# A 31-tap depthwise convolution on three engines or on TensorE, with its modulations moved the other way

## The chip, the cores and the metric

The kernel runs on one core of a Trainium2 chip. The metric is the device time of one execution in microseconds (us), the median of several runs. Five engines work side by side, each on its own instruction stream in order: TensorE (PE; its weight loads are shown apart as PEld), VectorE (DVE), ScalarE (ACT), GpSimd (POOL) and SyncE (SP), which here does nothing but issue DMAs. Instructions wait for each other by semaphores.

## The reference, cut to what matters

The program is a two-layer decoder trunk: 256 tokens, 2048 channels, float32. Layer 0 mixes tokens with a convolution module, layer 1 with attention; each is followed by a gated feed-forward block. The change concerns layer 0's mixer and the modulations around it.

```python
shift, scale, gate = jnp.split(silu(c) @ w + b, 3)          # adaLN, w is 2048 x 6144
h = rms_norm(x, g) * (1.0 + scale) + shift
u = h @ pw1_w + pw1_b                                       # 2048 -> 4096
val, gt = jnp.split(u, 2, axis=-1)
u = val * sigmoid(gt)
u = causal_depthwise_conv(u, dw_w, dw_b)                    # 31 taps, per channel
u = silu(layer_norm(u, ln_g, ln_b))
x = x + gate * (u @ pw2_w + pw2_b)
```

## The kernel before, in words

Activations lie channels on partitions, tokens along the row: 16 tiles of 128 x 256. A product keeps 128 x 128 blocks of weights stationary and streams 256 tokens. Float32 accuracy comes from splitting: ScalarE rounds a weight piece to a high part `wh` (L213), VectorE subtracts to get a low part `wl` (L214), and TensorE takes three products per block, `wh`\*`hh`, `wh`\*`hl`, `wl`\*`hh` (L251, L252, L253), at the fast fp32r rate. A piece is 8 blocks, 512 KB. `pieces` (L217) loads and splits ahead: after the first 16 pieces of pw1, five pieces of loads and three of splits.

All loads go through one queue on SyncE in the order in which the program writes them (`load`, L194). The buffers set when each can be issued: six for raw pieces (`raw`), three of 1 MB for modulation weights (`mraw`).

pw1 has 64 pieces. In the first 16 (called the head here) eight output blocks run at once, one piece for each channel tile kt. Each kt needs its scale and shift first: two 1 MB loads, two sums on VectorE over rows of 2048 (L276), then the modulated tile and its two parts (`start_tiles`, L498; `modulate_tile`, L354). GpSimd also rebuilds a full float32 tile `hf` (L506). The other 48 pieces run one output block after another, value and gate blocks of a tile in turn, so 4 pieces finish a tile. Of these 48, every fourth is "plain": not split, one float32 product a block (L249) on `hf`.

When a tile is finished, `pw1_done` (L517) computes `u` and starts a convolution (`conv`, L531), a generator that is advanced between pieces. Of the 31 taps, 12 are multiplied by ScalarE (L541) and added by GpSimd (L543, L545), 18 are multiply-adds on VectorE into a PSUM bank (L549), one is ScalarE's start (L535); VectorE joins both sums (L552). `y_sum` and `y_square` (L560, L579) give mean and variance over channels by products with a constant matrix (L569, L583).

Between the pieces run the steps of `mods0` (L482), the modulations that come next: the gate of this mixer, then scale and shift of the feed-forward. `mod_rows` (L455) sums them on TensorE, 1 MB a step, four products of 32 columns by 512 at a time (L466); only the last 1 MB loads go to VectorE (`mod_part`, L289). The rate is 0.6 steps a piece in pw1 (L31) and in pw2.

After pw1 the LayerNorm ends (L600 to L626): the last convolutions, the last sums, then pw2 (256 blocks) can start.

Of the kernel before, what the change touches and what calls it, by code (L numbers as in the profile page):

```python
# [17 lines left out]
PB = 8  # 128x128 blocks of weights in a piece  # L18
# [7 lines left out]
PRODUCTS = 8       # buffers between ScalarE and GpSimd  # L26
# [10 lines left out]
def plan(nbs, kts, first, stagger=4):  # L37
    """Order of the (output block, contraction tile) pairs of a product."""
# [9 lines left out]
class Cfg:  # L48
    def __init__(self, D, T, H, F, CW, FW):
# [3 lines left out]
        self.GH = 4  # L53
        self.rows0 = min(ROWS, KD // 4 - 1)

# [15 lines left out]
        items = [("c", KD), ("mix_g0", KD), ("mix_b0", 3 * KD), ("pw1_b", 2 * KD), ("cdw", KD * CW), ("cdb", KD), ("ln_g", KD), ("ln_b", KD),  # L71
# [6 lines left out]
        pl["pw1"] = plan(pairs, kd, min(8, 2 * KD), 0)  # L78
# [29 lines left out]
def hybrid_trunk(ctx: ExitStack, tc: tile.TileContext, cfg: Cfg, io: dict):  # L108
# [28 lines left out]
    # ---------------------------------------------------------------- constants and activations  # L137
# [53 lines left out]
    plain = {("pw1", i) for i in range(KD, 4 * KD) if i % PLAIN[0] == PLAIN[1]} if KD > 8 else set()  # L191
# [13 lines left out]
    def split_next():  # L205
        """High and low parts, of 12 significant bits each, of the next piece of weights."""
        blocks, v, n = raws[len(parts)]
        if stream[len(parts)] in plain:
            parts.append((blocks, v, None))
            return  # L210
# [6 lines left out]
    def pieces(name):  # L217
        """The pieces of a plan; loads and splits run ahead, over the ends of the plans."""
# [15 lines left out]
    def gemm(name, xh, xl, done, after=None, banks=(), x=None, width=None):  # L234
        """Weights stationary: psum[128 outputs, T] for each output block; done(block, psum)."""
        set_rate(name)
        left, ps, banks = {}, {}, list(banks)
        for nb, _ in cfg.plans[name]:
            left[nb] = left.get(nb, 0) + 1
        for blocks, wh, wl in pieces(name):  # L240
            for b, (nb, kt) in enumerate(blocks):
                first = nb not in ps
                if first:
                    ps[nb] = (banks.pop(0) if banks else psum_acc)()
# [3 lines left out]
                if wl is None:  # L248
                    nc.tensor.matmul(o, wh[:, c], x[kt], start=first, stop=left[nb] == 0)  # L249
                else:  # L250
                    nc.tensor.matmul(o, wh[:, c], xh[kt], start=first, stop=False)  # L251
                    nc.tensor.matmul(o, wh[:, c], xl[kt], start=False, stop=False)  # L252
                    nc.tensor.matmul(o, wl[:, c], xh[kt], start=False, stop=left[nb] == 0)  # L253
# [113 lines left out]
    class Entry:  # L367
# [585 lines left out]
```

## Time and profile before

| | |
|---|---|
| runs (3), us | 2379.94, 2383.69, 2388.55 |
| median | 2383.69 us |
| span of the profiled execution, first to last instruction | 2373.7 us |
| median less that span | 10.0 us |
| instructions | 45095 |
| TensorE busy / weight loads | 2280.7 / 2194.9 us |
| VectorE, ScalarE, GpSimd busy | 1814.1, 1219.0, 335.1 us |
| bytes moved by DMA, mean rate | 603.62 MB, 254 GB/s |

The profile holds one execution; the time of a run also contains some 10 us before the first and after the last instruction. A group row reads: line, engine, operation, output<-inputs, shapes, count, then busy time and mean duration of one instruction in ns, then the idle time before them and what ended it. A timeline row reads: start, length, engine, line, operation, count of merged instructions. A float32 product of TensorE appears as two records, an fp32r product as one. Matmuls overlap in the pipeline, so what one costs is the step from start to start, not its duration. A window row gives busy time and count of each engine, then the clock granted to TensorE, the busy share of the DMA engines and the rate.

### The profile page before, as it was taken

The numbers are of one execution on the slowest core, as the hardware profiler recorded it, in microseconds if no ns is written. First come the engines' busy times: TensorE is split into PE (matmuls) and PEld (weight loads), VectorE is DVE, ScalarE is ACT, GpSimd is POOL, SyncE is SP. The second block draws the span as 40 slices with busy tenths as digits, with TensorE's granted clock in tenths as the row PEclk, the third lists the DMA queues.
The fourth block names the chain that finished last, engine by engine and source line by source line (L and its number), as shares of the span: only waits on it lengthen the run. The fifth ranks groups of instructions, "written<-read, shape, count | busy, mean of one in ns | idle before, by whom it ended". The sixth has DMA issues, their size and how long they took to land.

```text
span 2373.7 us, 45095 instructions
## 1 busy us (share of the span) xinstructions
PE 2280.7 (96%) x18228; PEld 2194.9 (92%) x18228; DVE 1814.1 (76%) x2470; ACT 1219.0 (51%) x1828; POOL 335.1 (14%) x357
## 2 busy tenths in 40 slices
PE   5689989999999999999999999999999999999997
PEld 4677859999999999999998999999999999999997
DVE  8978988898878788788887667789876555666644
ACT  3266667665553345555465544556555434555443
POOL 2368652300000000000121000121000000000011
PEclk8799999999999999999999999999999999999999
DMA  8987879677769877778866676676865555566663
GB/s 341 350 342 279 299 261 354 209 264 282 274 249 354 311 275 291 265 278 322 317 239 241 240 254 238 239 250 260 292 216 187 187 187 187 187 188 187 188 186 105
DMA packets 138308, 603.62 MB, mean 254 GB/s; under 512 B 15346, under 2 KB 15474, under 8 KB 113522
## 3 DMA queue, kind: packets, MB, share of 16 engines
q1 hardware_dynamic: 138098, 600.74, 71.5%
q8 instruction: 142, 2.33, 0.4%
q14 instruction: 68, 0.55, 0.1%
HBM read 598.58 MB, written 2.10 MB: 253 GB/s over the span
## 4 chain that ended last, share of the span: by engine, by line
PE 82%; DVE 10%; issue 2%; POOL 2%; DMA 2%; ACT 2%; DVEq 0%; SPq 0%; POOLq 0%; ACTq 0%
PE ps L252 25%; PE ps L251 25%; PE ps L253 25%; DVE mraw L276 3%; DVE wl L214 2%; POOL y L545 2%; DMA mraw<-in_mt_ffn 1%; PE ps L787 1%; PE ps L788 1%; PE ps L789 1%; PE ps L249 1%; DVE auxb L549 1%; PE auxa L466 1%; DVE t L363 0%; DVE hl L321 0%
## 5 line engine op out<-in xcount | busy, mean ns | idle before, releaser
L213 ACT CAST wh<-raw 128x1024 fp32r<-128x1024 f32 x740 | 773.8, 1048 | 884.9 <-PE ps L252 652.1
L214 DVE TENSOR_TENSOR wl<-raw,wh 128x1024 fp32r<-128x1024 f32 x740 | 910.2, 1234 | 379.0 <-ACT wh L213 372.0
L251 PE MATMUL ps<-hh,wh 128*128 128x256 f32 (+1 forms) x3696 | 1036.6, 284 | 49.2 <-ACT hh L320 48.1
L252 PE MATMUL ps<-hl,wh 128*128 128x256 f32 (+1 forms) x3696 | 1044.1, 283 | 4.0 <-DVE hl L318 2.0
L253 PE MATMUL ps<-hh,wl 128*128 128x256 f32 (+1 forms) x3696 | 1039.0, 281 | 6.3 <-DVE wl L214 6.3
L251 PEld LDWEIGHTS ps<-hh,wh 128*128 128x128 f32 x3696 | 694.2, 190 | 63.0 <-ACT hh L320 52.5
L252 PEld LDWEIGHTS ps<-hl,wh 128*128 128x128 f32 x3696 | 709.2, 192 | 9.3 <-issue 3.4
L253 PEld LDWEIGHTS ps<-hh,wl 128*128 128x128 f32 x3696 | 704.2, 191 | 11.5 <-DVE wl L214 7.3
L252 PE MATMUL ps<-gl,wh 128*128 128x256 f32 x1408 | 396.2, 281 | 0.0
L251 PE MATMUL ps<-gh,wh 128*128 128x256 f32 x1408 | 396.2, 281 | 0.0
L253 PE MATMUL ps<-gh,wl 128*128 128x256 f32 x1408 | 396.2, 281 | 0.0
L276 DVE CUSTOM_DVE_ANT_0 mraw<-mraw,csr 128x2048 f32<-128x2048 f32 x152 | 347.6, 2287 | 56.2 <-DMA mraw<-in_mt_ffn 34.8
L336 POOL TENSOR_TENSOR sumsq<-sumsq,t 128x256 f32<-128x256 f32 x56 | 70.2, 1254 | 1570.4 <-ACT t L332 1570.1
L252 PEld LDWEIGHTS ps<-gl,wh 128*128 128x128 f32 x1408 | 265.0, 188 | 0.0
L251 PEld LDWEIGHTS ps<-gh,wh 128*128 128x128 f32 x1408 | 265.0, 188 | 0.0
L253 PEld LDWEIGHTS ps<-gh,wl 128*128 128x128 f32 x1408 | 265.0, 188 | 0.0
L656 DVE SCALAR_TENSOR_TENSOR t<-ps,par,t 128x254 f32<-128x254 f32 x336 | 160.4, 479 | 4.1
L545 POOL TENSOR_TENSOR y<-y,prod 128x256 f32<-128x256 f32 x160 | 144.4, 911 | 12.9 <-ACT prod L541 3.0
L549 DVE SCALAR_TENSOR_TENSOR auxb<-u,cpar,auxb 128x256 f32<-128x256 f32 x288 | 118.8, 481 | 1.1 <-ACT auxb L535 0.9
L541 ACT ACTIVATE prod<-u,cpar 128x256 f32<-128x256 f32 x192 | 85.5, 500 | 40.3 <-DVE u L528 24.1
L653 ACT ACTIVATE t<-ps,par 128x256 f32<-128x256 f32 x168 | 93.9, 560 | 0.0
L332 ACT ACTIVATE t<-x 128x256 f32<-128x256 f32 x75 | 30.1, 414 | 85.9 <-DVE x L676 37.0
(174 smaller groups left out, 2107.9 us busy)
## 6 DMA issues: line engine op xcount, KB each, us to landing
raw<-in_w_down SPq DMA_DIRECT2D x176, 512.0 KB, 4.3
mraw<-in_mt_mix SPq DMA_DIRECT2D x80, 1024.0 KB, 7.3
mraw<-in_mt_ffn SPq DMA_DIRECT2D x72, 1024.0 KB, 6.7
raw<-in_w_pw SPq DMA_DIRECT2D x96, 512.0 KB, 6.2
raw<-in_w_up01b SPq DMA_DIRECT2D x84, 512.0 KB, 4.9
raw<-in_w_up11b SPq DMA_DIRECT2D x84, 512.0 KB, 3.5
raw<-in_w_up00b SPq DMA_DIRECT2D x80, 512.0 KB, 4.6
raw<-in_w_up10b SPq DMA_DIRECT2D x80, 512.0 KB, 3.6
```

Source lines behind the costliest of these rows:

```text
L213: nc.scalar.copy(wh[:, :n], v[:, :n])
L214: nc.vector.tensor_tensor(wl[:, :n], v[:, :n], wh[:, :n].bitcast(F32), op=ALU.subtract)
L251: nc.tensor.matmul(o, wh[:, c], xh[kt], start=first, stop=False)
L252: nc.tensor.matmul(o, wh[:, c], xl[kt], start=False, stop=False)
L253: nc.tensor.matmul(o, wl[:, c], xh[kt], start=False, stop=left[nb] == 0)
L276: nc.vector.tensor_tensor_reduce(out=v, in0=v, in1=csr, scale=1.0, scalar=0.0, op0=ALU.mult, op1=ALU.add, accum_out=macc[:, nb:nb + 1])
L336: engine.tensor_tensor(self.sum, self.sum, sq, op=ALU.add)
L541: nc.scalar.activation(pr, u[:, i:i + T], AF.Copy, scale=tap(i))
L545: nc.gpsimd.tensor_tensor(y, y, pr, op=ALU.add)
L549: nc.vector.scalar_tensor_tensor(o, u[:, k:k + T], tap(k), o, op0=ALU.mult, op1=ALU.add)
L653: nc.scalar.activation(y, ps[:, :T], AF.Identity, bias=pc(f"fdb{i}", nb, 1), scale=w(FW - 1))
L656: nc.vector.scalar_tensor_tensor(y[:, s:], ps[:, :T - s], w(k), y[:, s:], op0=ALU.mult, op1=ALU.add)
```

## The change

The convolution moves to TensorE. For each channel tile the 128 channels are cut into four blocks of 32; for block i a buffer `wide` holds four copies of its `u`, each on 32 partitions and shifted by 0 to 3 tokens. One product with a 128 x 32 matrix of taps then does four taps of 32 channels; eight such products, 4 tokens apart, do the 31 taps (one tap is zero), and the four blocks go to the four column groups of the array: 32 float32 products of 128 x 32 by 256 a tile, 512 in all. The copies are made by DMA: 16 issues for each group of two tiles (the last two tiles are groups of one), on the same SyncE queue, in program order. GpSimd builds the tap matrices, ScalarE adds the bias while it copies the result out.

In return the modulations go to VectorE: all of `mods0` but 8 steps runs as `mod_part`, at 1.06 steps a piece instead of 0.6. No piece of pw1 is plain any more, so `hf` is gone. Value and gate of a tile share one PSUM bank (`gemm_pairs`). In the head, GpSimd multiplies x by 1/rms for all tiles in advance and ScalarE applies scale and shift, where VectorE did both in one instruction.

```diff
-POOL_TAPS = 12     # conv taps that ScalarE multiplies and GpSimd adds; VectorE has the others
-CONV_PACE = 0.7    # steps of the running convolutions after each piece
-PLAIN = (4, 3)     # of each 4 pieces of pw1, the one that goes to TensorE as float32, unsplit
-PW1_RATE, BUBBLE, LN_STEPS = 0.6, 8, 7
+HEAD = 8
+SH = 4
+CONV_PACE = 1.25
+PW1_RATE, BUBBLE, LN_STEPS = 1.06, 8, 7
...
+                mm = [(wh, xh), (wh, xl), (wl, xh)]
+                for k, (w, x) in enumerate(mm):
+                    nc.tensor.matmul(o, w[:, c], x[kt], start=first and k == 0, stop=left[j] == 0 and k == 2,
+                                     skip_group_check=True)
...
         def mods0():
-            yield from mod_rows("mix0", 2 * KD // 4, KD // 4)
+            yield from mod_part("mix0", 2)
             nc.vector.tensor_tensor(gb, modv["mix0"][:, 2 * KD:3 * KD], pc("pw2_b"), op=ALU.mult)
-            have.add(("mix0", 2))
-            yield from mod_rows("ffn0", KD // 4, KD // 4)
-            mod_scale("ffn0", 0, KD)
-            have.add(("ffn0", 1))
+            yield from mod_part("ffn0", 1)
             if cfg.rows0:
                 yield from mod_rows("ffn0", 0, cfg.rows0)
             yield from mod_part("ffn0", 0, 4 * cfg.rows0)
...
+        for kt in range(KD):
+            nc.gpsimd.tensor_tensor(ys[kt], xs[kt], rs, op=ALU.mult)
...
-                hh[kt], hl[kt] = modulate_tile("mix0", kt, rs)
-                nc.gpsimd.tensor_tensor(hf[kt], hh[kt].bitcast(F32), hl[kt].bitcast(F32), op=ALU.add)
+                hh[kt], hl[kt] = [v[:, :T] for v in h_tiles(kt)]
+                t = t256()
+                nc.scalar.activation(t, ys[kt], AF.Identity, bias=modv["mix0"][:, kt:kt + 1],
+                                     scale=moda["mix0"][:, kt:kt + 1])
+                split_act(t, hh[kt], hl[kt])
...
+        def conv(g, u):
+            n = len(g)
+            v = wide[groups.index(g) % 2]
+            for s in range(SH):
+                for i in range(SH):
+                    load(u[i * C32:(i + 1) * C32, :n, :], v[s * C32:(s + 1) * C32, i, :n, PADW - s:PADW - s + T])
+            taps = []
+            for j in g:
+                t = cpool2.tile([P, SH * NM, C32], F32, name="taps", bufs=3)
+                w = pc("cdw", j * SH * NM, SH * NM)
+                nc.gpsimd.tensor_tensor(t, w.unsqueeze(2).to_broadcast([P, SH * NM, C32]),
+                                        pc("eye").unsqueeze(1).to_broadcast([P, SH * NM, C32]), op=ALU.mult)
+                taps.append(t)
+            yield
+            yield
+            for a, j in enumerate(g):
+                o = psum_b()[:, :T]
+                for m in range(NM):
+                    for i in range(SH):
+                        nc.tensor.matmul(o[i * C32:(i + 1) * C32, :], taps[a][:, i * NM + m, :],
+                                         v[:, i, a, SH * m:SH * m + T], start=m == 0, stop=m == NM - 1,
+                                         tile_position=(0, i * C32))
+                    if m == NM // 2 - 1:
+                        yield
+                nc.scalar.activation(ys[j], o, AF.Identity, bias=pc("cdb", j, 1))
+                late.append(j)
+                yield
```

How the instructions stand. First SyncE at the end of the head, before: behind the last modulation loads and the parameters come five raw pieces at once (`mt` are modulation weights that VectorE sums, `mr` those that TensorE sums).

```order
L195 DMA mraw<-in_mt_mix 128x2048 x2
L195 DMA raw<-in_w_pw 128x1024
L195 DMA par<-in_params 128x912
L195 DMA cst<-in_consts 128x144
L195 DMA raw<-in_w_pw 128x1024 x5
L195 DMA mraw<-in_mr_mix 128x2048
L195 DMA raw<-in_w_pw 128x1024 x2
```

The same place on SyncE in the changed kernel:

```order
L194 DMA mraw<-in_mt_mix 128x2048 x2
L194 DMA raw<-in_w_pw 128x1024
L194 DMA par<-in_params 128x912
L194 DMA cst<-in_consts 128x144
L194 DMA wide_218<-u 32x2x256 x16
L194 DMA wide_219<-u 32x2x256 x16
L194 DMA mraw<-in_mt_mix 128x2048
L194 DMA raw<-in_w_pw 128x1024 x5
```

The 32 copies of the first two groups, which read `u` and so wait for the end of the head's products, now stand ahead of the five raw pieces.

Second, SyncE of the changed kernel at the end of pw1 (names with their buffer numbers; `wide1` takes tile 14, `wide0` tile 15, the last):

```order
L194 DMA raw_3031<-in_w_pw1 128x1024
...
L194 DMA wide1_219<-u_3129 32x256 x16
L194 DMA mraw_3168<-in_mt_ffn0 128x2048
L194 DMA raw_3172<-in_w_pw2 128x1024
L194 DMA mraw_3203<-in_mt_ffn0 128x2048
L194 DMA raw_3206<-in_w_pw2 128x1024
L194 DMA mraw_3253<-in_mt_ffn0 128x2048
L194 DMA raw_3256<-in_w_pw2 128x1024
L194 DMA mraw_3303<-in_mt_ffn0 128x2048
L194 DMA raw_3307<-in_w_pw2 128x1024
L194 DMA wide0_218<-u_3337 32x256 x16
```

Between the last weights of pw1 (the first row) and the copies of the last tile stand five modulation loads of 1 MB and five pieces of pw2 (one of each in the two rows left out); before, no DMA stood between the last tile of pw1 and its convolution.

Third, TensorE of the changed kernel after the head, where before the split products ran on with a four-product modulation step about every second piece (`hh`, `hl` and `wl` as above, `taps` the tap matrices):

```order
L268 MATMUL ps<-hh_561,wl 128x256
L568 MATMUL auxb<-wide_218,taps 32x256 x32
L591 MATMUL ps<-y_186,ones_d 128x256
L568 MATMUL auxb<-wide_219,taps 32x256 x2
L568 MATMUL auxb<-wide_218,taps 32x256
L568 MATMUL auxb<-wide_219,taps 32x256
L568 MATMUL auxb<-wide_218,taps 32x256 x4
L568 MATMUL auxb<-wide_219,taps 32x256 x29
L568 MATMUL auxb<-wide_218,taps 32x256 x11
L568 MATMUL auxb<-wide_219,taps 32x256 x5
L268 MATMUL ps<-hh_606,wh 128x256
```

After one piece behind the head, 85 convolution products come in a block; later groups come as blocks of 64, three to five pieces behind the end of their tiles.

More of the change, by code (lines that the diff above doesn't have):

```diff
@@ L53, in __init__ @@
         self.GH = 4
+        self.NM = -(-CW // SH)
         self.rows0 = min(ROWS, KD // 4 - 1)
@@ L531, in conv @@
[L531 to L553 removed]
+        groups = [list(range(j, min(j + 2, KD - 2))) for j in range(0, KD - 2, 2)] + [[KD - 2], [KD - 1]]
@@ new lines, in hybrid_trunk, with pw1_done @@
+        group_of = {j: g for g in groups for j in g}
+        wide = [cpool2.tile([P, SH, 2, PADW + T], F32, name=f"wide{i}") for i in range(2)]
+        for v in wide:
+            nc.gpsimd.memset(v[:, :, :, :PADW], 0.0)
+            nc.gpsimd.memset(v[:, :, :, PADW + T - SH + 1:], 0.0)
+        u_of = {}
+        def pw1_done(j, ps):
+            g = group_of[j]
+            if j == g[0]:
+                u_of[j] = cpool2.tile([P, 2, T], F32, name="u", bufs=5)
+            u = u_of[g[0]][:, j - g[0], :]
+            sg = t256()
+            nc.scalar.activation(sg, ps[:, T:2 * T], AF.Sigmoid, bias=pc("pw1_b", j + KD, 1))
+            nc.vector.scalar_tensor_tensor(u, ps[:, :T], pc("pw1_b", j, 1), sg, op0=ALU.add, op1=ALU.mult)
+            if j == g[-1]:
+                side.append(conv(g, u_of.pop(g[0])))
```

110 lines of the change are left out of this document (39 added, 71 removed).

## The prediction

> **What bounds the kernel now.** I read the page's busy times first, then the windows, cut at the borders of layer 0's stages, then the groups of TensorE and VectorE in each stage, then timelines where one operation's price is needed.
>
> ```profile
> PE 2280.7 (96%) x18228; PEld 2194.9 (92%) x18228; DVE 1814.1 (76%) x2470; ACT 1219.0 (51%) x1828; POOL 335.1 (14%) x357
> ```
>
> TensorE bounds the whole; the change touches only the first 455 us. The window rows are the head, the other 48 pieces of pw1 (the stage below), the gap to pw2, and pw2:
>
> ```profile
> 20.00:139.50 119.50, 75.61 (x381) 71.22 (x382) 114.84 (x157) 26.00 (x34) 41.46 (x16) 0.74 0.93 350
> 139.50:324.60 185.10, 181.37 (x1308) 147.98 (x1310) 162.69 (x324) 125.74 (x242) 144.00 (x157) 1.00 0.80 295
> 324.60:357.90 33.30, 25.11 (x129) 10.76 (x121) 29.18 (x67) 20.15 (x47) 15.03 (x19) 0.94 0.68 254
> 357.90:455.40 97.50, 97.50 (x808) 93.61 (x809) 85.90 (x136) 65.13 (x123) 23.68 (x14) 0.98 0.84 307
> ```
>
> In the head VectorE is busy 114.8 of 119.5 us, DMA at a share of 0.93: both near their limits. In the stage TensorE is busy 181 of 185 us; VectorE (163) has room. pw2 is all TensorE.
>
> The stage's TensorE groups:
>
> ```profile
> L251 PE MATMUL ps<-hh,wh 128*128 128x256 f32 x288 | 83.7, 291 | 1.1 <-ACT wh L213 1.1
> L252 PE MATMUL ps<-hl,wh 128*128 128x256 f32 x288 | 81.2, 282 | 0.0
> L253 PE MATMUL ps<-hh,wl 128*128 128x256 f32 x288 | 80.9, 282 | 2.1 <-DVE wl L214 2.1
> L249 PE MATMUL ps<-hf,raw 128*128 128x256 f32 x192 | 44.7, 382 | 0.0
> L466 PE MATMUL auxa<-mraw,hot 128*32 128x512 f32 x219 | 29.2, 604 | 0.6 <-DMA mraw<-in_mr_mix 0.6
> L569 PE MATMUL ps<-y,ones_d 128*128 128x256 f32 x20 | 5.2, 384 | 0.0
> ```
>
> Their prices come from starts. The first two rows below are 27 split products apart; then come a plain piece and the product after it; then the last product before a modulation step, the step, and the product after it:
>
> ```profile
> 254.75 0.28 PE L253 MATMUL ps<-hh,wl 128*128 128x256 f32 x1
> 257.89 0.28 PE L253 MATMUL ps<-hh,wl 128*128 128x256 f32 x1
> 259.89 3.72 PE L249 MATMUL ps<-hf,raw 128*128 128x256 f32 x16
> 263.26 0.47 PE L251 MATMUL ps<-hh,wh 128*128 128x256 f32 x1
> 266.16 0.28 PE L253 MATMUL ps<-hh,wl 128*128 128x256 f32 x1
> 266.36 1.06 PE L466 MATMUL auxa<-mraw,hot 128*32 128x512 f32 x8
> 267.36 0.39 PE L251 MATMUL ps<-hh,wh 128*128 128x256 f32 x1
> ```
>
> A split product costs 3.14 / 27 = 0.1163 us, so a piece (24) 2.79; a plain piece 3.37; a modulation step 1.20 less one normal step of 0.12 = 1.08. The stage adds up: 36 x 2.79 + 12 x 3.37 + 27.4 steps x 1.08 + 10 sums x 0.52 = 176 us, and 3.8 us of waits; 5 of the 185 stay unexplained. So TensorE's list of work is the stage's length.
>
> **The change, part by part.** *Head.* VectorE's work for one kt:
>
> ```profile
> 61.26 2.28 DVE L276 CUSTOM_DVE_ANT_0 mraw<-mraw,csr 128x2048 f32<-128x2048 f32 x1
> 68.75 2.29 DVE L276 CUSTOM_DVE_ANT_0 mraw<-mraw,csr 128x2048 f32<-128x2048 f32 x1
> L363 DVE SCALAR_TENSOR_TENSOR t<-x,a_mix,rstd 128x256 f32<-128x256 f32 x11 | 5.3, 485 | 0.4
> ```
>
> One kt lasts 7.5 us (first row to second, two sums each). L363's 0.485 goes, and L321 gets about 0.06 shorter. The DMA share of 0.93 allows 7 per cent more, about the same. 15 kt x 0.5 = -7 us (bounds 0, if DMA holds the pace, and -8).
>
> *TensorE's list in the stage.* Plain pieces: 12 x (2.79 - 3.37) = -7. Modulation steps: 27.4 become 8, -19.4 x 1.08 = -21. Three more channel sums: +1.6. The convolution is new; its nearest row is L466, the same form with 512 columns where it has 256. A run of it in the gap, first the products, then the weight loads:
>
> ```profile
> 339.24 2.78 PE L466 MATMUL auxa<-mraw,hot 128*32 128x512 f32 x22
> 339.69 0.13 PEld L466 LDWEIGHTS auxa<-mraw,hot 128*32 128x32 f32 x4 [0.30 <-issue]
> 340.12 0.13 PEld L466 LDWEIGHTS auxa<-mraw,hot 128*32 128x32 f32 x4 [0.30 <-issue]
> 340.55 0.12 PEld L466 LDWEIGHTS auxa<-mraw,hot 128*32 128x32 f32 x3 [0.30 <-issue]
> ```
>
> Four records, one in each column group, take 0.43 us together. With half the columns 0.215; a tile has 64 records, 16 fours, 3.44 us. Fifteen tiles fall in the stage: 52 us, and 2 us for ten blocks' edges (a step's 1.08 less its 0.86 of streaming). The bounds: not below 52, since the columns must stream; above, one record at the pace of any product and load seen, 64 x 0.1163 = 7.4 us a tile, +59. I take 54, the same form's. Sum: -7 - 21 + 1.6 + 54 = +27.6, less the 3.8 us of old waits: **+24**.
>
> The weight loads decide whether 3.44 holds: in the rows above the four loads (0.13) start as the next four products are already streaming. The Trainium skill (TensorE: Matmul & The Clock Gate, Part 3, The mechanism) states that a weight load overlaps products in flight only if it goes to other row groups; here every load fills all rows, so by that rule none is hidden. The rows above disagree: the loads of 339.69 and 340.12 cost no time beyond the streaming.
>
> *The head's end.* Before, SyncE issued the next weights while the head still ran:
>
> ```profile
> 124.93 0.62 SPq L195 DMA_DIRECT2D cst<-in_consts  x1
> 125.65 6.21 SPq L195 DMA_DIRECT2D raw<-in_w_pw  x5
> 1.20 1.78 SPq L195 DMA_DIRECT2D x<-in_xT  x4
> DMA to landing us min/median/max: 3.3/4.8/12.2
> ```
>
> Now 32 copies stand there. They wait for u of tile 1, that is for the head's last products (near 132), and an issue costs 1.78 / 4 = 0.44 us: 14 us in which no weights are issued. The next piece is split near 151. Meanwhile TensorE has one piece (2.8) and 85 convolution products (9): of some 19 us, **+7** stays idle (bounds 0, if issue and landing go at the fastest, and 9).
>
> *Transfers in the stage.* The same orders add mods at 1.06 a piece. From the head's end to pw1's last weights SyncE issues 47 pieces, 41 modulation loads and 5 groups of copies: 25 + 43 + 5 = 73 MB in about 200 us, 365 GB/s. Before, the stage moved 295 at a share of 0.80, so full would be 369. TensorE and DMA are level, and the copies cost DMA more than their bytes: their issues rotate over eight semaphores, so the eighth copy waits until the load ahead of it has landed, and the next load waits for the ninth copy. That drains the queue: a landing of 3.3 us and two or three issues, about 4.5 us a group, five times. While five pieces lie ahead, TensorE has 14 us of cover and loses nothing; without that lead it pays each time. I take **+3** (0 to 15). The Trainium skill (DMA: Bandwidth & Descriptors, Specifications) gives HBM about 358 GB/s per core; by that the 73 MB would last 204 us, and the 3 would be some 8. The head's 350 agrees; a 20 us stretch in pw2 had more:
>
> ```profile
> 400.00:420.00 20.00, 20.00 (x172) 20.00 (x171) 20.00 (x28) 10.38 (x18) 6.44 (x3) 1.00 1.00 397
> ```
>
> The other engines' rows, of the whole span:
>
> ```profile
> L214 DVE TENSOR_TENSOR wl<-raw,wh 128x1024 fp32r<-128x1024 f32 x740 | 910.2, 1234 | 379.0 <-ACT wh L213 372.0
> L545 POOL TENSOR_TENSOR y<-y,prod 128x256 f32<-128x256 f32 x160 | 144.4, 911 | 12.9 <-ACT prod L541 3.0
> L549 DVE SCALAR_TENSOR_TENSOR auxb<-u,cpar,auxb 128x256 f32<-128x256 f32 x288 | 118.8, 481 | 1.1 <-ACT auxb L535 0.9
> L541 ACT ACTIVATE prod<-u,cpar 128x256 f32<-128x256 f32 x192 | 85.5, 500 | 40.3 <-DVE u L528 24.1
> ```
>
> VectorE gets 33 sums of 2.28 (75 us) and 12 splits of 1.23 (15) in the stage, and loses the 288 multiply-adds (119, nearly all there): nothing on the path, with room left. ScalarE loses 85 us. GpSimd's additions (911 ns for 256 columns) make way for tap matrices of 1024, some 3.6 us a tile by the same rate, while a tile of pw1 takes 11 us or more: hidden; without that cover it would be 3.6 us a tile.
>
> *Gap.* The last u, the last join of sums, and pw2's first products:
>
> ```profile
> 325.54 0.48 DVE L528 SCALAR_TENSOR_TENSOR u<-ps,cpar,t 128x256 f32<-128x256 f32 x1
> 347.75 0.42 DVE L552 TENSOR_TENSOR y<-y,auxb 128x256 f32<-128x256 f32 x1
> 357.89 1.22 PE L251 MATMUL ps<-zh,wh 128*128 128x256 f32 x4 [0.95 <-ACT zh L317]
> ```
>
> From u to join 22 us, join to pw2 9.7. Now: 16 issues (7), landing (3.3), 3.4 of products, a copy out (0.6): 14 instead of 22, -8, if the queue is free. But the last copies stand behind five 1 MB loads and five pieces, 8 MB, which end 22 us after pw1's last weights; TensorE is 5 to 14 us behind those weights, so the copies come 8 to 17 us after its last product of pw1, and not at 10. I take **-2** (-10 to +6).
>
> *pw2.* 768 products x 0.1163 = 89.3 against 97.5; what goes with the modulations (L466, four steps in pw2):
>
> ```profile
> L466 PE MATMUL auxa<-mraw,hot 128*32 128x512 f32 x32 | 4.3, 605 | 0.0
> ```
>
> Four steps of 1.08, their bias products 1, and the start's slower clock stays: **-7.5** taken (bounds -5 and -8).
>
> Behind pw2 nothing changes. Sum: -7 + 24 + 7 + 3 - 2 - 7.5 = +17.5. On the profiled span: 2373.7 + 17.5 = 2391.2; runs lie 10 us over the span (median 2383.7), so **2401 us**.
>
> **The rivals.** *Everything overlaps.* Five pieces of lead return quickly, copies wait for nothing: hole 4, drains 0, gap -9, so -7 + 24 + 4 - 9 - 7.5 = +4.5, 2388 us. For it: share 0.80 before, and pieces 17 to 21 come without modulations between. Against: 365 of 369 GB/s.
>
> *Faster.* The mechanism is VectorE's relief at the borders. If the 5 us that the stage's list leaves unexplained are VectorE's late splits and sums, they go with its load: TensorE +19. The hole closes, because 85 products and a piece cover the loads; the gap gives 10, the head 8, pw2 8, and the blocks' edges of 2 us overlap: -8 + 17 + 0 - 10 - 8 = -9, 2375 us. It decides at the head's end: the first piece behind the copies must be split by the time the 85 products end. Against it: only 3.8 us of waits are on record in the stage.
>
> *Weight loads not hidden under 256 columns.* Under 512 columns a load of 0.13 has 0.43 to hide in; under 256 only 0.215, and twice as many loads for the time. If each four pays it: 256 x 0.13 = +33, 2434 us. The rows speak against it.
>
> That the change would not do what it says is excluded: the orders show the 512 products and the copies.
>
> **How the numbers follow.** The forecast (TensorE's longer list and SyncE's copies) gets 0.55: the list is counted and priced by rows of the same forms. Overlap 0.19, faster 0.15, unhidden loads 0.11. A measurement of this kernel tells about 0.3 per cent, 7 us, from no change: 2376.5 to 2390.8 is the same. Faster: 0.15. Same: the overlap's 0.19 and 0.04 of the forecast's low end, 0.23. Slower: 0.51 + 0.11 = 0.62. The range goes from 2378, which leaves out most of the faster case, to 2434, the unhidden loads' time, which leaves out half of them; between them lie the forecast's bounds (hole 0, drains 0, gap -10: 2383; drains 15, gap +6: 2421).
>
> **What would show it.** In the changed profile: kt steps of 7.0 in the head; 32 copies on SyncE near 132 to 146 and TensorE idle some 7 us before 151; four records in 0.215 and 3.4 us a tile; in the stage's waits, TensorE waiting for splits that wait for raw pieces, and SyncE for copies; a stage of 210 to 225 us; a gap of about 31; pw2 in 90. I am wrong if the stage takes under 200 us, or if the tile's products take 7 us.

## The result, and the profile after

The changed kernel takes 2455.4 us (median of 4 runs, 2452.3 to 2457.3), the kernel before 2383.8 beside it: the ratio is 1.031, with a 95% interval of 1.0287 to 1.0333. The forecast of 2401 had the sign right and less than a quarter of the size.

First the page's busy times, to set beside the line of before:

```profile
PE 2320.0 (94%) x19076; PEld 2235.5 (91%) x19076; DVE 1786.1 (73%) x2226; ACT 1158.5 (47%) x1662; POOL 194.8 (8%) x196
```

TensorE is busy 39 us longer, and the span is 82 us longer: about half of the loss is work, the other half waiting. Where, the windows say, cut at the same borders as before (the head's last products, the last product of pw1, first and last product of pw2; columns as in the prediction):

```profile
20.00:137.40 117.40, 75.43 (x385) 70.90 (x386) 112.51 (x146) 36.10 (x53) 28.03 (x16) 0.78 0.86 331
137.40:393.40 256.00, 224.34 (x2150) 183.65 (x2148) 155.34 (x142) 63.81 (x84) 35.53 (x13) 0.97 0.82 302
393.40:437.90 44.50, 22.22 (x166) 13.29 (x164) 28.75 (x48) 16.42 (x40) 0.00 (x0) 0.79 0.69 264
437.90:532.40 94.50, 94.46 (x768) 94.43 (x769) 67.56 (x109) 63.24 (x106) 12.35 (x14) 0.97 0.56 167
```

| part | before, us | after, us | predicted change | measured change |
|---|---|---|---|---|
| head, from 20 us | 119.5 | 117.4 | -7 | -2.1 |
| stage (48 pieces of pw1) | 185.1 | 256.0 | +24 + 7 + 3 = +34 | +70.9 |
| gap to pw2 | 33.3 | 44.5 | -2 | +11.2 |
| pw2 | 97.5 | 94.5 | -7.5 | -3.0 |
| behind pw2 | 1918.3 | 1923.1 | 0 | +4.8 |
| span | 2373.7 | 2455.5 | +17.5 | +81.8 |

The profiled spans differ by 81.8 us and the medians by 71.6. The profiled run of after took 2457.3 us, 1.8 over its span, and the later runs of the kernel before lie 1.7 over theirs (2379.89 and 2378.2 us, for one). So the 10 us between the span of before and its median are not time outside the span, as the text ahead of the prediction has it: that profile shows one of the shorter runs. The 4.8 us behind pw2, where nothing changed, may come from that.

The stage is the place. Its waits on TensorE, which were 3.8 us before (line, what it waited for, total, times, longest):

```profile
PE ps L268 <- DVE wl L210: 13.6, 20, 1.4
PE auxb L568 <- DMA wide<-u: 11.9, 3, 7.5
PE ps L268 <- ACT wh L209: 2.8, 4, 1.3
```

In all it sat idle for 31.7 of the 256.0 us. Late splits (`wl`, `wh`) wait in turn for raw pieces. Why these are late is on SyncE's timeline: all the copies of the first four tiles with the weights behind them, and two later groups.

```profile
137.90 21.14 SPq L194 DMA_DIRECT2D wide<-u  x32
159.77 3.13 SPq L194 DMA_DIRECT2D raw<-in_w_pw  x5
...
275.25 15.64 SPq L194 DMA_DIRECT2D wide<-u  x16
317.63 15.29 SPq L194 DMA_DIRECT2D wide<-u  x16
```

Sixteen copies keep SyncE for over 15 us in four of the stage's five groups of two tiles (11.3 in the first), and a group lasts 42 us (275.25 to 317.63). The duration of one issue, minimum, median and maximum over a group's sixteen, in ns, and how long a copy takes to land (last column, us):

```profile
L194 SPq DMA_DIRECT2D wide<-u x16: 585/594/598, 233.7 to 248.8; - x16
wide<-u SPq DMA_DIRECT2D x112, 64.0 KB, 2.0
```

So 16 x 0.64 us from start to start is 10.2 us of issuing, and the other 5 are pauses: in the group that begins at 233.69 the issues stop twice, behind 237.95 and behind 240.65, for 2.1 and 2.4 us, until a load eight places ahead has landed (eight places ahead of the copy at 243.66 stands the piece issued at 233.22, which landed after 10.4 us, at 243.6).

```profile
237.95 0.59 SPq L194 DMA_DIRECT2D wide<-u  x1
240.65 0.58 SPq L194 DMA_DIRECT2D wide<-u  x1
243.66 1.86 SPq L194 DMA_DIRECT2D wide<-u  x3
```

What this does to the DMA engines shows in two windows, the transfers between two groups of copies and the copies behind them (last two columns: DMA share, GB/s):

```profile
216.40:233.00 16.60, 15.70 (x126) 15.12 (x126) 16.51 (x14) 5.16 (x6) 3.60 (x2) 1.00 1.02 415
234.00:249.00 15.00, 12.38 (x94) 11.36 (x94) 10.87 (x12) 3.53 (x4) 0.00 (x0) 1.00 0.75 229
```

The queue takes turns: 15 us at little over half the rate, then 26 us near the full rate (390 GB/s from 249.5 to 275.2). A group is the sum of the two, 42 us; the copies run ahead of nothing, since the loads that should overlap them stand behind them in the same order.

### The profile page after: what moved, and what is told of

It reads as the page before. It is cut to its first block, busy times and chain, and to the rows that moved or that the text cites. A ratio compares the mean times of both kernels' runs of the same rounds, so it can differ in the third digit from the quotient of the medians.

```text
span 2455.5 us, 46380 instructions
## 1 busy us (share of the span) xinstructions
PE 2320.0 (94%) x19076; PEld 2235.5 (91%) x19076; DVE 1786.1 (73%) x2226; ACT 1158.5 (47%) x1662; POOL 194.8 (8%) x196
## 4 chain that ended last, share of the span: by engine, by line
PE 77%; DVE 8%; DMA 8%; issue 3%; SPq 2%; ACT 1%; POOL 0%; DVEq 0%; ACTq 0%; POOLq 0%
PE ps L245 23%; PE ps L244 23%; PE ps L246 23%; DMA raw<-in_w_pw 3%; DVE mraw L291 3%; DMA mraw<-in_mt_ffn 3%; DVE wl L210 3%; SPq L194 2%; PE ps L268 2%; DMA mraw<-in_mt_mix 2%; PE auxb L568 1%; PE ps L812 1%; PE ps L811 1%; PE ps L813 1%; DVE hl L333 1%
## 5 line engine op out<-in xcount | busy, mean ns | idle before, releaser
L210 DVE TENSOR_TENSOR wl<-raw,wh 128x1024 fp32r<-128x1024 f32 x752 | 928.2, 1239 | 404.8 <-ACT wh L209 398.3
L245 PE MATMUL ps<-hl,wh 128*128 128x256 f32 (+1 forms) x3328 | 931.8, 280 | 3.5 <-DVE hl L333 2.0
L244 PE MATMUL ps<-hh,wh 128*128 128x256 f32 (+1 forms) x3328 | 934.5, 281 | 0.1
L246 PE MATMUL ps<-hh,wl 128*128 128x256 f32 (+1 forms) x3328 | 928.0, 279 | 6.2 <-DVE wl L210 6.2
L245 PEld LDWEIGHTS ps<-hl,wh 128*128 128x128 f32 x3328 | 631.1, 190 | 4.4 <-DVE hl L333 2.5
L244 PEld LDWEIGHTS ps<-hh,wh 128*128 128x128 f32 x3328 | 625.8, 188 | 0.8 <-DVE x L835 0.3
L291 DVE CUSTOM_DVE_ANT_0 mraw<-mraw,csr 128x2048 f32<-128x2048 f32 x184 | 427.5, 2324 | 143.6 <-DMA mraw<-in_mt_ffn 78.0
L351 POOL TENSOR_TENSOR sumsq<-sumsq,t 128x256 f32<-128x256 f32 x56 | 59.1, 1055 | 1626.0 <-ACT t L347 1620.3
L268 PE MATMUL ps<-hh,wh 128*128 128x256 f32 x416 | 122.4, 310 | 44.9 <-ACT hh L332 41.7
L268 PE MATMUL ps<-hh,wl 128*128 128x256 f32 x416 | 131.4, 317 | 13.7 <-DVE wl L210 13.6
L268 PEld LDWEIGHTS ps<-hh,wh 128*128 128x128 f32 x416 | 84.3, 210 | 53.4 <-ACT hh L332 45.8
L268 PE MATMUL ps<-hl,wh 128*128 128x256 f32 x416 | 130.6, 315 | 0.1
```

The costliest lines, as they stand in the source:

```text
L210: nc.vector.tensor_tensor(wl[:, :n], v[:, :n], wh[:, :n].bitcast(F32), op=ALU.subtract)
L268: nc.tensor.matmul(o, w[:, c], x[kt], start=first and k == 0, stop=left[j] == 0 and k == 2, skip_group_check=True)
L291: nc.vector.tensor_tensor_reduce(out=v, in0=v, in1=csr, scale=1.0, scalar=0.0, op0=ALU.mult, op1=ALU.add, accum_out=macc[:, nb:nb + 1])
L351: engine.tensor_tensor(self.sum, self.sum, sq, op=ALU.add)
```

## The experiments

The theories were S (SyncE's copies hold up the weights), T (TensorE's longer list is the loss), B (the DMA engines lack the bandwidth) and G (GpSimd's new work slows VectorE in the head). The runs were made in three sets and stand here by question; the kernel before took 2381.1, 2380.5 and 2382.1 us beside the sets.

### What paces the stage: no copies, or few products

`no_copies`:

```diff
-            for s in range(SH):
-                for i in range(SH):
-                    load(u[i * C32:(i + 1) * C32, :n, :], v[s * C32:...])
...
+            nc.gpsimd.memset(v, 0.0)
```

> The 144 copies of u are left out (the products read a buffer of zeros, so the convolution's result is wrong; everything else is as in the changed kernel, 2455 us). Theory S: SyncE, which issues 16 copies at 0.64 us each and drains its queue in between, is kept some 15 us per group from issuing weights and modulations, and a group of two tiles then lasts 42 us where TensorE's own list for it is about 34: without copies the stage shortens by some 12 us at the head's end and 5 x 8 us behind it, the gap by about 15: 2390 us, 2380 to 2400. Theory T: TensorE's list is longer and its products slower than costed, the copies are mostly beside it: only the hole and the gap shrink, 2430 us or more. Theory B: DMA bandwidth is the limit, the copies' own 1 MB a group is what they cost: 2440 us or more.

Measured: 2408.3 us, ratio 1.0117 (1.0101 to 1.0133), 47 us less than the changed kernel. The stage takes 220.5 us and the gap 21:

```profile
145.60:366.10 220.50, 219.67 (x2024) 169.06 (x2023) 149.51 (x156) 60.13 (x82) 18.76 (x9) 1.00 0.83 314
366.10:387.20 21.10, 8.32 (x37) 6.67 (x36) 19.22 (x25) 13.24 (x28) 0.00 (x0) 0.78 0.89 327
```

TensorE is busy 220 of 220.5 us. So the copies cost more than half of the loss, and what stays without them is TensorE's list: S and T each hold a part, and the time lies between theirs. One thing is not as in the changed kernel: without copies to wait for, the products of the first four tiles (256 records) ran in the head. These 128 products are some 14 us at the 0.109 us found below, and the head ended 8 us later for them (at 145.6 instead of 137.4 us), so on balance this run flatters the kernel without copies by some 6 of the 47 us.

`few_products`:

```diff
-                for m in range(NM):
+                for m in (0, NM - 1):
...
-                    if m == NM // 2 - 1:
+                    if m == 0:
```

> 8 of the 32 convolution products of a tile are left (two of the eight tap groups), the copies and all else stay; the convolution's result is wrong. It takes some 3.5 us a tile off TensorE, 53 us in the stage. Theory S (SyncE's copies pace the stage): TensorE only waits longer, the group still lasts about 42 us; 2440 us, 2430 to 2455. Theory T (TensorE's list): the time falls by most of the 53: 2400 to 2415 us. Theory B (DMA bandwidth): as S, 2440 or more.

Measured: 2450.5 us, ratio 1.0293 (1.0277 to 1.0309). Three quarters of the new products are gone, and the time falls by 5 us. From one piece behind the head to the end of pw1 it takes 251.9 us, the changed kernel 253.2; SyncE's groups stay at 42, and TensorE waits instead:

```profile
275.96 16.92 SPq L194 DMA_DIRECT2D wide<-u  x16
317.60 16.48 SPq L194 DMA_DIRECT2D wide<-u  x16
```

```profile
PE ps L268 <- DVE wl L210: 18.7, 19, 3.9
PE auxb L568 <- DMA wide<-u: 16.3, 3, 7.6
PE ps L268 <- ACT wh L209: 13.3, 9, 3.5
```

In the changed kernel the copies' pace, and not the list, sets the stage. (At 0.109 us a product the run takes 2.6 us a tile off TensorE, 39 in fifteen tiles, and not the 53 expected; theory T would still have had some 2416 us.)

### Who issues the copies

`copies_on_act`, and in the second set `copies_on_pool`:

```diff
-                    load(u[...], v[...])
+                    tc.keep_in_program_order(nc.scalar.dma_start(v[...], u[...]))    # copies_on_act
+                    tc.keep_in_program_order(nc.gpsimd.dma_start(v[...], u[...]))    # copies_on_pool
```

> The same copies, issued by ScalarE's instruction stream instead of SyncE's: the same bytes, descriptors and products. Theory S: SyncE goes on issuing weights while the copies run, at the price of some 10 us a group in which ScalarE splits nothing: 2415 us, 2395 to 2435. Theory T and theory B: the same as the changed kernel, 2445 to 2465.

Measured: 2489.3 us, ratio 1.0457 (1.0438 to 1.0477), slower still. The expectation was wrong by 74 us: it priced ScalarE's standstill at the issues alone. On ScalarE's timeline the copies of the first four tiles, and the split behind them:

```profile
140.81 30.88 ACTq L554 DMA_DIRECT2D wide<-u  x30
171.73 2.94 ACT L209 CAST wh<-raw 128x1024 fp32r<-128x1024 f32 x3 [30.01 <-DMA wide<-u]
```

ScalarE splits nothing for 30 us. The copies now share the DMA engines with the loads and land after 5.6 us (median) instead of 2.0.

> The same 16 copies a group, issued by GpSimd's instruction stream, which has nothing else to do there but the tap matrices: SyncE is free of them and no engine that computes is held up; the bytes are the same. Theory S (SyncE held up by issues and drains): groups follow at the pace of TensorE's list, 36 us for 42, the hole closes: 2415 us, 2400 to 2430. Theory B (the copies and the modulations need more of the DMA engines than they have): the same as the changed kernel or little better, 2440 to 2460.

Measured: 2463.2 us, ratio 1.0346 (1.0330 to 1.0362). SyncE is free, nobody who computes stands still, and nothing is gained. In the page the copies' landing, then TensorE's one wait in the stage:

```profile
wide<-u POOLq DMA_DIRECT2D x112, 64.0 KB, 7.4
```

```profile
PE auxb L568 <- DMA wide<-u: 34.9, 6, 8.7
```

Here the copies take as long by landing late as they took on SyncE by being issued slowly: GpSimd issues eight of a group in 4.3 us and then waits for landings (the group of 193.44 has its ninth issue at 200.07). The products, whose place in TensorE's order is fixed, wait for them. The gap falls to 31.8 us, but the stage grows by some 17. S as it was worded failed here: freeing SyncE gained nothing, and the time alone would speak for B. The next two runs separate the number of issues (I) from the bytes (B).

### Issues or bytes

`tiny_copies` keeps the sixteen issues and drops the bytes; `four_issues` keeps the bytes and drops the issues:

```diff
-                    load(u[i * C32:(i + 1) * C32, :n, :], v[s * C32:(s + 1) * C32, i, :n, PADW - s:PADW - s + T])
+                    load(u[i * C32:(i + 1) * C32, :n, :4], v[s * C32:(s + 1) * C32, i, :n, PADW - s:PADW - s + 4])
...
-                for i in range(SH):
-                    load(u[i * C32:(i + 1) * C32, :n, :], v[s * C32:(s + 1) * C32, i, :n, PADW - s:PADW - s + T])
+                load(u[:, :n, :], v[:, s, :n, PADW - s:PADW - s + T])
...
+            nc.gpsimd.memset(v, 0.0)          # in both
```

> The same 16 copies a group on SyncE, but of 4 columns a tile instead of 256: as many issues and descriptors, one 64th of the bytes (the rest of the buffer stays zero, the convolution's result is wrong). Theory I (the issues: 16 x 0.64 us on SyncE, and its waits for the loads eight places ahead, stop the stream of weights): a group still takes about 15 us of SyncE and 40 to 42 in all: 2445 us, 2435 to 2458. Theory B (the copies' bytes: they keep the DMA engines 5 us a group or more, which the loads lack): the groups come at TensorE's pace: 2415 to 2430.

> The reverse: the same bytes in descriptors of the same size, in 4 copies of 128 partitions a group instead of 16 of 32 partitions (blocks land in the wrong place, the convolution's result is wrong). Theory I: SyncE is held for 4 issues of some 0.6 to 1 us, and no issue waits for the loads: the hole shrinks to 3 to 5 us, a group to 36, the last copies come 12 us earlier: 2415 us, 2405 to 2430. Theory B: the same bytes, the same 42 us a group; only the hole gets shorter: 2440 to 2455.

Measured: `tiny_copies` 2445.8 us, ratio 1.0279 (1.0261 to 1.0296); `four_issues` 2421.9 us, ratio 1.0174 (1.0156 to 1.0191). Both lie in theory I's ranges and outside theory B's. A 64th of the bytes gains 10 us, a quarter of the issues 34. SyncE with tiny copies (two groups), then with four issues (three groups):

```profile
233.73 14.10 SPq L194 DMA_DIRECT2D wide<-u  x16
276.03 11.90 SPq L194 DMA_DIRECT2D wide<-u  x16
```

```profile
223.50 3.07 SPq L194 DMA_DIRECT2D wide<-u  x4
259.41 4.64 SPq L194 DMA_DIRECT2D wide<-u  x4
295.40 3.20 SPq L194 DMA_DIRECT2D wide<-u  x4
```

A tiny copy is issued no faster than a full one (median 0.594 us for both), so sixteen still take 12 to 14 us. Four copies take 3 to 5 us, the groups follow every 36 us instead of every 42, the hole nearly closes, and the gap is 30.1 us. What the sixteen issues themselves cost (10 of a group's 15 us) and what the pauses between them (5), these runs do not separate.

### GpSimd in the head

`no_pool_in_head`:

```diff
-        for kt in range(KD):
-            nc.gpsimd.tensor_tensor(ys[kt], xs[kt], rs, op=ALU.mult)
...
-                nc.scalar.activation(t, ys[kt], AF.Identity, bias=...)
+                nc.scalar.activation(t, xs[kt], AF.Identity, bias=...)
...
-    cput("cdw", taps...)          # lands early
+    put("cdw", taps...)           # lands behind the head
```

> GpSimd's work is taken out of the head: the multiplication of x by 1/rms for all tiles is left out (ScalarE scales x itself, so the result is wrong) and the first tap matrices are made from a later table of parameters, after the head. Theory G: GpSimd's 28 us of multiplications and 6 us of taps slow the VectorE instructions beside them (2.28 becomes 2.81 us a sum), which delayed the first product from 23.2 to 27.7 us and the first four channel tiles by 1.3 us each: the head ends some 9 us earlier, 2446 us. Rival: the head's pace is set by DMA or by ScalarE's longer chain, and stays: 2452 to 2459.

Measured: 2440.2 us, ratio 1.0247 (1.0230 to 1.0265), 15 us less. The head ends 6 us earlier, not 9 (the last product before the first wait for copies starts at 134.09 us instead of 140.09). The two profiled spans differ by 11.0 us, of which the other 5 lie behind the head, 3.1 of them behind pw2, where nothing differs; so only some 6 of the 15 us are shown to be the head's. VectorE's first sums of some channel tiles, in the changed kernel with GpSimd's row beside them, then without its work:

```profile
22.15 28.03 POOL L510 TENSOR_TENSOR y<-x,rstd 128x256 f32<-128x256 f32 x16 [5.84 <-DVE rstd L366]
28.40 2.81 DVE L291 CUSTOM_DVE_ANT_0 mraw<-mraw,csr 128x2048 f32<-128x2048 f32 x1
36.48 0.84 DVE L333 TENSOR_TENSOR hl<-t,hh 128x256 fp32r<-128x256 f32 x1
37.24 2.81 DVE L291 CUSTOM_DVE_ANT_0 mraw<-mraw,csr 128x2048 f32<-128x2048 f32 x1
```

```profile
23.80 2.29 DVE L291 CUSTOM_DVE_ANT_0 mraw<-mraw,csr 128x2048 f32<-128x2048 f32 x1
29.99 0.43 DVE L333 TENSOR_TENSOR hl<-t,hh 128x256 fp32r<-128x256 f32 x1
30.33 2.28 DVE L291 CUSTOM_DVE_ANT_0 mraw<-mraw,csr 128x2048 f32<-128x2048 f32 x1
```

While GpSimd multiplies, a tile takes VectorE 8.84 us (28.40 to 37.24); without it 6.53 (23.80 to 30.33), and the second tile begins 4.6 us earlier. Most of these 4.6 us belong to the early tap matrices: VectorE's fourteen sums of squares at the start (L351) took 11.86 us in the changed kernel, where GpSimd built taps from 10.03 to 16.31 us, and 7.31 in `change_best` below, which moves the taps and keeps the multiplications. There the second tile begins at 24.46 us and the last at 124.28; in the changed kernel the last begins at 128.38, without taps and multiplications at 119.11. So on VectorE the taps cost some 4 us and the multiplications some 5. (Both runs also load 272 KB less of parameters ahead of the head, which is not separated.)

The Trainium skill (SBUF — State Buffer, SBUF: two separate sides) states that VectorE and GpSimd share a pair of ports as an exclusive lock, which a GpSimd instruction, or against one that reads SBUF a VectorE one with two inputs in SBUF, holds to its end. The rows agree: the same instruction took 0.84 us instead of 0.43. The waiting goes the other way too. In the kernel before, an addition of GpSimd that started 0.16 us behind a sum on VectorE (61.26, in the prediction) took 2.71 us, and 0.73 while VectorE did nothing:

```profile
61.42 2.71 POOL L506 TENSOR_TENSOR hf<-hh,hl 128x256 f32<-128x256 f32 x1 [4.79 <-DVE hl L321]
136.45 0.73 POOL L506 TENSOR_TENSOR hf<-hh,hl 128x256 f32<-128x256 f32 x1 [4.79 <-DVE hl L321]
```

That the lock is the cause, and not something else that the two engines' running together brings with it, no run here separates.

### Other deliveries, and a version that beats both

`copies_by_scalar`, in which ScalarE computes the copies itself, and `rate_06`:

```diff
-                    load(u[...], v[...])
...
+            for s in range(SH):
+                for i in range(SH):
+                    nc.scalar.copy(v[s * C32:(s + 1) * C32, i, :n, PADW - s:PADW - s + T], u[i * C32:(i + 1) * C32, :n, :])
+                yield
...
-PW1_RATE, BUBBLE, LN_STEPS = 1.06, 8, 7
+PW1_RATE, BUBBLE, LN_STEPS = 0.6, 8, 7
```

> No DMA at all for the copies: ScalarE copies u itself, 32 partitions by two tiles an instruction, four between two pieces; about 0.5 us each, 16 a group, 8 us of a ScalarE that is busy 63 of 254 us in the stage. Theory S and theory T together (without SyncE's copies TensorE's own list of some 220 to 227 us is the bound): stage 225 to 232, gap 25 to 30, 2410 us, 2400 to 2420. Theory B: the same, as the copies' bytes are gone too, so only the kernel with GpSimd's issues tells S from B. Rival: ScalarE, held up by 8 us of copies a group, is late with the splits: 2430 or more.

Measured: 2427.7 us, ratio 1.0199 (1.0185 to 1.0212), 28 less than the changed kernel and 18 more than expected. A copy costs 571 ns:

```profile
L561 ACT COPY wide<-u 32x512 f32<-32x512 f32 (+1 forms) x144 | 82.2, 571 | 7.0 <-DVE u L545 4.9
```

The stage takes 240.7 us, the gap 31.6. TensorE's recorded waits in the stage are 14 us: 7 in front of the first convolution products, 7 for splits. The rival of late splits has some part in it.

> The changed kernel with 0.6 modulation steps a piece of pw1, as before the change, instead of 1.06: per group 4.8 MB of modulations instead of 8.5, all else the same; the rest of them falls into pw2. Theory B (bytes pace the groups): a group's 13.5 MB become 9.8, so TensorE's list (36 us for 42) is what is left: 2420 to 2430. Theory S: a group is 15 us of copies and the transfers between them, 27 us for 11 MB; these get shorter too, to some 20, so about the same gain, but the hole and the gap stay: 2425 to 2435. Theory T (TensorE's list alone): no gain, 2450 to 2460. Rival: the modulations left over hold up pw2's end: 2455 or more.

Measured: 2431.5 us, ratio 1.0212 (1.0197 to 1.0226). The stage falls to 218.7 us and the groups to 32, but pw2 rises to 103.8 and the gap stays at 46.1. Fewer loads in the queue also mean fewer pauses between the copies: a group's sixteen take 10 to 13 us. The time lies in S's range and 1.5 us above B's, too near to tell them apart; it is the 42 us sum of copies and transfers, shortened at its other end.

`change_best` puts these two and the late tap matrices together:

> What is left of the change's cost when its copies are delivered well: ScalarE makes the copies (2428 us alone), the modulations run at 0.6 steps a piece again (2431 alone), and the tap matrices are built after the head from the later table. If TensorE's longer list is what remains: stage 225, gap 30, head 4 us shorter: 2414 us, 2405 to 2422, still slower than the kernel before. Rival: with the splits and transfers out of the way the stage falls to the 205 us of its list and the total to the kernel before's: 2385 to 2395.

Measured: 2413.9 us, ratio 1.0148 (1.0129 to 1.0167), as expected: stage 228.9, gap 30.3, head 3 us shorter (it ends at 134.5 instead of 137.4). With its deliveries mended, the change still costs 32 us.

`before_with_new_head` is the kernel before with one idea of the change, `before_paced_head` the same with GpSimd's multiplications spread:

```diff
-                hh[kt], hl[kt] = modulate_tile("mix0", kt, rs)
-                nc.gpsimd.tensor_tensor(hf[kt], hh[kt].bitcast(F32), hl[kt].bitcast(F32), op=ALU.add)
+                hh[kt], hl[kt] = [v[:, :T] for v in h_tiles(kt)]
+                if kt > 1:                                                       # before_paced_head only
+                    nc.gpsimd.tensor_copy(hf[kt][:, :1], macc[:, kt - 2:kt - 1])
+                nc.gpsimd.tensor_tensor(hf[kt], xs[kt], rs, op=ALU.mult)
+                nc.scalar.activation(hf[kt], hf[kt], AF.Identity, bias=..., scale=...)
+                split_act(hf[kt], hh[kt], hl[kt])
```

> The kernel before, with one idea of the change: in the head ScalarE applies scale and shift to an x that GpSimd has multiplied by 1/rms for all tiles in advance, into the full tile itself, so GpSimd's addition of the two parts is gone. Theory G: VectorE's step for a channel tile falls from 7.5 to 6.6 us where GpSimd is idle (16 tiles, 14 us), and GpSimd's 28 us of multiplications at the start cost about 9 of them: 2376 us, 2371 to 2381, against 2381 for the kernel before. Rival (the head is paced by DMA or by something else than VectorE): no difference, or slower by the 9 us.

> The kernel before with the new head once more, but GpSimd's multiplications by 1/rms are spread, one for each channel tile, each behind the sum of two tiles ahead, instead of all in the first 28 us. Theory G (a VectorE instruction that meets a running GpSimd one waits for part of it): each tile's step is 7.0 to 7.1 us from the start, the head ends some 2 us earlier than with all of them in front: 2374 us, 2370 to 2378. Rival (the meeting costs each tile what the 28 us cost together): 7.5 us a tile, 2381.

Measured: 2377.1 us, ratio 0.9983 (0.9973 to 0.9993), and 2377.4 us, ratio 0.9982 (0.9970 to 0.9994): both beat both kernels, by a narrow 0.2 per cent. In the first a tile takes up to 8.85 us while GpSimd is busy and mostly 6.6 afterwards; in the second mostly 7.05 from the third tile on, as theory G said. Over the head the two come to the same (the last tile's first sum starts at 124.25 and 124.63 us, 128.78 in the kernel before), so spreading gains nothing.

## Why the prediction was wrong, point by point

Its terms beside the measured ones, which add up to the 81.8 us between the two spans; the stage's change of 70.9 is taken apart by what TensorE waited for:

| term | predicted, us | measured, us |
|---|---|---|
| head | -7 | -2.1 |
| TensorE's list, less the old waits | +24 | +39.2 |
| hole at the head's end | +7 | +12.4 |
| drains (all other waits of the stage) | +3 | +19.3 |
| gap | -2 | +11.2 |
| pw2 | -7.5 | -3.0 |
| behind pw2 | 0 | +4.8 |

**The drains, +3 (0 to 15): the step that failed.** It read: "That drains the queue: a landing of 3.3 us and two or three issues, about 4.5 us a group." The pauses are there and last some 5 us. What the step left out is the sixteen issues themselves, which the text had counted for the head's end (14 us) and for the gap (7 us) but not for the five groups in between. A group holds SyncE for some 15.5 us and not 4.5, more than the 14 us that five pieces of lead cover. The 358 GB/s of the Trainium skill (DMA: Bandwidth & Descriptors, Specifications) was no limit: 415 passed in the window of 16.6 us above. The waits behind the hole, nearly all for splits and for later copies, are 19 us of TensorE's time, and `four_issues` gets 34 us back in the drains, the hole and the gap together.

**SyncE's price of an issue, 0.44 us.** It was taken from loads of x with 128 partitions, the nearest row then. A copy takes 0.64 from start to start. In the hole at the head's end that made 21 us of copies out of 14. The copies did open the hole, but by another wait than the prediction's late weights: TensorE stood mostly for the copies themselves, ahead of its first convolution products:

```profile
147.91 7.02 PE L568 MATMUL auxb<-wide,taps 128*32 128x256 f32 x64 [7.54 <-DMA wide<-u]
155.49 0.70 PE L591 MATMUL ps<-y,ones_d 128*128 128x256 f32 x2 [0.56 <-ACT y L573]
158.70 8.62 PE L568 MATMUL auxb<-wide,taps 128*32 128x256 f32 x106 [2.52 <-DMA wide<-u]
170.57 0.39 PE L268 MATMUL ps<-hh,wl 128*128 128x256 f32 x1 [1.36 <-DVE wl L210]
```

With a wait of 0.4 between the last two rows these are 12.4 us idle, where +7 (0 to 9) stood: 10.1 for copies, 1.7 for splits of late weights, 0.6 for a channel sum's input. The idle time has a second price, unforeseen: the granted clock was 0.65 from 148 to 155 us.

**The gap, -2 (-10 to +6): measured +11.2.** The last copies did stand behind the loads, 10 us after the last u, as the text had it; but their issue took 17.3 us, not 7, and the products behind them 7.0, not 3.4:

```profile
393.88 0.48 DVE L545 SCALAR_TENSOR_TENSOR u<-ps,cpar,t 128x256 f32<-128x256 f32 x1 [1.30 <-ACT t L544]
404.09 17.32 SPq L194 DMA_DIRECT2D wide<-u  x16
420.94 7.01 PE L568 MATMUL auxb<-wide,taps 128*32 128x256 f32 x64 [10.58 <-DMA wide<-u]
437.94 0.80 PE L244 MATMUL ps<-zh,wh 128*128 128x256 f32 x2 [7.07 <-ACT zh L332]
```

With four issues the gap is 30.1 us, 3 less than before: the term was right but for the issues.

**TensorE's list, +24: the product's price held.** A run of 64 products (two tiles) with all its copies landed, in the run at rate 0.6, and a run of eight in `no_copies`, each between its neighbours:

```profile
243.27 0.28 PE L268 MATMUL ps<-hh,wl 128*128 128x256 f32 x1
243.48 7.17 PE L568 MATMUL auxb<-wide,taps 128*32 128x256 f32 x128
250.57 0.39 PE L268 MATMUL ps<-hh,wh 128*128 128x256 f32 x1
```

```profile
305.95 0.28 PE L268 MATMUL ps<-hh,wl 128*128 128x256 f32 x1
306.17 1.07 PE L564 MATMUL auxb<-wide,taps 128*32 128x256 f32 x16
307.17 0.38 PE L268 MATMUL ps<-hh,wh 128*128 128x256 f32 x1
```

From 7.30 = 0.12 + 64p + e and 1.22 = 0.12 + 8p + e follow p = 0.109 us and an edge e of 0.23, to which the slower step behind it adds 0.1. A tile is 32p = 3.5 us; 3.44 was predicted. The rival of unhidden weight loads is out, though its 2434 came nearest, and the rule of the Trainium skill weighed there (TensorE: Matmul & The Clock Gate, Part 3, The mechanism) disagrees with these rows as with those of before. The edges are dearer than the 0.2 assumed. TensorE's busy time in the stage rose by 43 us (224.3 for 181.4) where +27.6 was listed for fifteen tiles; only fourteen had their products there (896 of the 1024 records), so some 19 us are over. About 14 of these lie in runs that start when the first copies have landed and then wait for the others: the two long rows above took 7.02 us for 32 products and 8.62 for 53, at 0.109 each 3.5 and 5.8, and four later two-tile runs some 9 us, a clean one 7.2. The edges explain some 3. That these runs wait for copies is not tried apart, but at rate 0.6, where four of five such runs took 7.2 to 7.6, the busy time is 201.5 (of the difference some 9 are the eight modulation steps, which fall behind pw1 there).

**The head, -7: measured -2.1.** A tile's step fell even further than predicted, to 6.6 us at best (7.0 predicted), once GpSimd was idle. But the multiplication by 1/rms, described ahead of the prediction, and the first tap matrices were given no price on VectorE; the taps delayed its start and the multiplications its first four tiles, and together they cost it the 9 us worked out above. Without both the head ends 6 us earlier. The prediction looked for GpSimd's cost on GpSimd alone.

**pw2, -7.5: measured -3.0.** The modulations did leave. The products ran at 0.12 us each, not at the stage's 0.1163, and pw2 started behind a wait, at a clock of 0.75 in its first 10 us.

**The other rivals.** "Everything overlaps" (2388) failed with the drains; even `change_best` is 26 us above it. "Faster" rested on VectorE's relief: VectorE's load in the stage fell (162.7 to 155.3 us), and TensorE had waited for it only 2.1 us. Of the two signs that were to prove the prediction wrong (a stage under 200 us, 7 us a tile) neither came: both watched the list, and the fault was in the queue.

The 71.6 us, as far as the runs show them one by one: some 34 for the number of issues, 15 in the run without GpSimd's work in the head (6 of them seen in the head), and 32 that stay in `change_best`, where TensorE is busy 33.8 us longer in the stage than in the kernel before (215.2 for 181.4). These overlap and do not add up exactly.

## What to carry to other kernels

Count every issue of a transfer as time of the queue that makes it, at each place where it occurs, and compare the sum with the lead that the queue's other loads have; a small copy cost as much to issue as a large one. When the issuer is changed, ask what else that engine does in order, and who then waits for the landing. Work moved to an idle engine is not free if a busy one beside it slows down: look at the busy one's durations, not at the idle one's row.

## What the runs showed of the hardware

- A copy within SBUF of 32 partitions took 0.594 us to issue on SyncE, with 64 KB or with 1 KB; one of 128 partitions with 256 KB took 0.608 (median). The number of issues counted, not their size.
- The same 64 KB copies landed after 2.0 us on SyncE's queue, which had drained before them, after 5.6 on ScalarE's and 7.4 on GpSimd's, which run beside the loads.
- A sum on VectorE of 2.28 us took up to 2.81 beside GpSimd's multiplications, a subtraction 0.84 for 0.42; in the kernel before, GpSimd's additions in the head left the sums at 2.28, but took 2.72 us each themselves, 0.73 while VectorE did nothing.
- After 7.5 us without a product TensorE's granted clock was 0.65 over the next 7 us.
